# One tile for nine weight buffers, with the feature-major weights 16 bytes further on

## Chip, core and metric

The kernel runs as one program on one core of a Trainium2 chip. The metric is the device time of one execution in microseconds; for the kernel before it is the median of three runs.

## What is computed

Two transformer blocks in fp32 for 256 tokens of width 2048. Nearly all of the work is matrix products of the 256 tokens with weights that are read once from HBM:

```python
# first block
h = rmsnorm(x, g_mix);  proj = h @ w_in
y_sb = stick_breaking_attention(...);  y_ca = chunked_relpos_attention(...)
merged = sigmoid(gate_sb) * (y_sb @ w_sb_out) + sigmoid(gate_ca) * (y_ca @ w_ca_out)
x = x + merged @ w_mix_out
h = rmsnorm(x, g_ffn);  g_ff, u_ff = split(h @ w_ffn_in)
x = x + (silu(g_ff) * u_ff) @ w_ffn_out
x = x + sigmoid(rmsnorm(x, g_ple) @ w_ple_gate) * (p @ w_ple_in)
# second block: s5, gated linear attention and differential attention side by side,
# merged through w_out, then a gated MLP with a convolution (w_up, w_down), a last rmsnorm
```

## The kernel before

**Precision.** Every large product is made of three passes in `float32r`. Weights and activations are each split into a high part (rounded to `float32r`) and a low part (the rest), and high by high, high by low and low by high are summed in PSUM.

**Halves.** All weights pass through one loop, `stream` (L450). A half is 128 x 1024 fp32 of a weight matrix, 512 KB; there are 1089. For each half a DMA on SP's queue fills one of four `raw` buffers (L460), ScalarE writes the high part `wh` (L467), and VectorE writes the low part `wl` (L477). The step of half `i` first issues the cast of half `i + 4` and the subtraction of half `i + 3`, which in its turn issues the load of the half that comes four after its own; then it issues the matmuls of half `i`, and then one tick of the generators that do everything else (attention, norms, evacuations). `wh` has five buffers and `wl` four, each 4 KB per partition, each pool's buffers side by side.

**Two kinds of job.** The activations lie as `x`: for each block of 128 features, 256 columns of high parts and then 256 of low parts (2048 bytes per partition).

- In a token-major job (kind "AS", `mm_as`, L561 to L563) the activations are the stationary operand (128 x 128, 512 bytes per partition) and the weights are moved through, 512 columns at a time. A half of it has twelve matmuls: low activations by `wh`, high by `wl`, high by `wh`, for two feature blocks and two blocks of tokens.
- In a feature-major job (kind "WS", L527 and L531) a 128 x 128 piece of the weights is stationary and the activations are moved through: `wh` against all 512 columns of `x` (L527, the high matmul), `wl` against its 256 high columns only (L531, the low matmul). A half has sixteen matmuls, in pairs of a low and a high one; a job has four halves, so 32 pairs. The feature-major matrices are the query and key projections, `w_fin`, `w_up`, `w_u` and `w_r`: 492 of the halves. They come in runs of 16 to 48 halves, with token-major halves between.

A single half (`w_alr`, kind "W4") is 128 x 512 and is used in plain fp32.

**Memory.** Pools lie one behind the other in SBUF: the activation slots, the pool `one` (with the parameters `par` in it, and behind them the constants `cst`), then `raw`, `wh`, `wl` and the scratch pool `ev`. `par` has 208 columns and is given 96 more that nothing uses. In the layout that follows from these sizes, each of the five `wh` and four `wl` buffers starts 256 bytes away, modulo 512, from where each 2048-byte block of activations starts.

Of the kernel before, what the change touches and what calls it, by code (L numbers as in the profile page):

```python
# [9 lines left out]
F32 = mybir.dt.float32  # L10
F32R = mybir.dt.float32r
# [12 lines left out]
CA = 4  # L24
SA = 3
COOL = 1
RAWB = 4


# [130 lines left out]
class Flag:  # L160


    def __init__(self, tile=None):
        self.tile, self.ready = tile, False
# [21 lines left out]
class Build:  # L186
    NSLOT = 15

    def __init__(self, tc, d, out, es):
        self.tc, self.nc, self.d, self.out = tc, tc.nc, d, out  # L190
        pool = lambda name, bufs, **kw: es.enter_context(tc.tile_pool(name=name, bufs=bufs, **kw))
        self.slotp, self.one = pool("slots", 1), pool("one", 1)
        self.rawp, self.whp, self.wlp = pool("raw", RAWB), pool("wh", CA + 1), pool("wl", SA + 1)
        self.ev = pool("ev", 2)
        self.accp = pool("acc", 2, space=PSUM)
        self.psp = pool("ps", 1, space=PSUM)
        self.drp = pool("dr", 1, space=bass.MemoryType.DRAM)
        self.psfree, self.cooling, self.ticks = [0, 1, 2, 3], [], 0
        self.slotfree = list(range(self.NSLOT))
        self.gens, self.lanes, self.nm = [], {}, 0  # L200
        self.tab, self.forced, self.nrb = None, 0, 0
# [43 lines left out]
    def unbank(self, b):  # L245
        self.cooling.append((self.ticks + COOL, b[1]))

# [201 lines left out]
    def stream(self, jobs):  # L449
        nc = self.nc  # L450
        halves = [(j, i, ks) for j in jobs for i, ks in j.halves]
        N = len(halves)
        raws, spl = {}, {}
        width = lambda j, ks: {"AS": 512 * len(ks), "WS": 1024, "W4": 512}[j.kind]

        def load(i):
            j, idx, ks = halves[i]
            n = width(j, ks)
            r = self.rawp.tile([128, 1024], F32, tag="raw", name=self.name("raw"))
            nc.sync.dma_start(out=r[:, :n], in_=self.d[j.w][idx][:, :n])  # L460
            raws[i] = r

        def high(i):
            j, idx, ks = halves[i]
            n = width(j, ks)
            wh = self.whp.tile([128, 1024], F32R, tag="wh", name=self.name("wh"))
            nc.scalar.copy(wh[:, :n] if j.kind != "W4" else wh[:, :n].bitcast(F32), raws[i][:, :n])  # L467
            spl[i] = wh

        def low(i):  # L470
            j, idx, ks = halves[i]
            n = width(j, ks)
            r, wh = raws.pop(i), spl[i]
            wl = None
            if j.kind != "W4":
                wl = self.wlp.tile([128, 1024], F32R, tag="wl", name=self.name("wl"))
                nc.vector.tensor_sub(wl[:, :n], r[:, :n], wh[:, :n].bitcast(F32))  # L477
            spl[i] = (wh, wl)
            if i + RAWB < N:
                load(i + RAWB)  # L480

        ahead = self.at_start(load)
        for i in range(CA):
            next(ahead)
            high(i)
            if i < SA:
                low(i)
        self.add(ahead)
        last, prev, acc = None, None, None
        for i, (j, idx, ks) in enumerate(halves):  # L490
            if i + CA < N:
                high(i + CA)
            if i + SA < N:
                low(i + SA)
            if j is not last:
                if j.before is not None:
                    j.before()
                while prev is not None and not prev.free:
                    self.tick(must=True)
                prev, last = last, j  # L500
                acc = self.accp.tile([128, 2, 512], F32, tag="acc", name=self.name("acc"))
            for k in ks:
                while k not in j.acts.ready:
                    self.tick(must=True)
            first, end = j.halves[0][1][0], j.halves[-1][1][-1]
            if j.by_m is not None:

                for m in range(2):
                    for q, (_, _, kq) in enumerate(halves[i:]):
                        self.mm_as(j.acts, kq, *spl[i + q], acc, (m,), first, end)  # L510
                    j.by_m(m, acc)
                break
            wh, wl = spl.pop(i)
            if j.kind == "AS":
                self.mm_as(j.acts, ks, wh, wl, acc, (0, 1), first, end, low_last=i == 0)
            elif j.kind == "W4":

                for k in range(16):
                    p = slice(32 * (k % 4), 32 * (k % 4) + 32)
                    nc.tensor.matmul(acc[p, 0, :], lhsT=wh[:, 32 * k:32 * k + 32].bitcast(F32),  # L520
                                     rhs=j.acts.at(k).bitcast(F32), start=k < 4, stop=k >= 12)
            else:
                for kk, k in enumerate(ks):
                    x = j.acts.at(k)
                    for f in range(2):
                        s = slice((kk * 2 + f) * 128, (kk * 2 + f) * 128 + 128)
                        hi = lambda: nc.tensor.matmul(  # L527
                            acc[:, f, :], lhsT=wh[:, s], rhs=x, start=k == first, stop=k == end)
                        if k == first:
                            hi()  # L530
                        nc.tensor.matmul(acc[:, f, 256:512], lhsT=wl[:, s], rhs=x[:, 0:256], start=False, stop=False)  # L531
                        if k != first:
                            hi()
            if i + 1 == N or halves[i + 1][0] is not j:
                self.add(j.evac(acc, lambda j=j: setattr(j, "free", True)), front=True)
            self.tick()
        while self.gens:
            self.tick(must=True)
# [40 lines left out]
    def consts(self):  # L579
        nc, d, one = self.nc, self.d, self.one  # L580

        self.par = one.tile([128, P_N + 96], F32, tag="par", name="par")[:, 0:P_N]
        self.cst = one.tile([128, C_N], F32, tag="cst", name="cst")
        nc.sync.dma_start(out=self.par, in_=d["par"])
        c = self.cst
        self.ident, self.ones, self.BT = (c[:, o:o + 128] for o in (C_ID, C_ONE, C_BT))
        self.one1 = c[:, C_ONE:C_ONE + 1]
# [14 lines left out]
    def first(self):  # L602
# [6 lines left out]
        def start(load):  # L609
# [4 lines left out]
            def load_xt(g):  # L614
                nc.sync.dma_start(out=xs[g // 4][0][:, (g % 4) * 2:(g % 4) * 2 + 2], in_=d["xt"][:, 2 * g:2 * g + 2])

            for g in range(RAWB):
                load_xt(g)
                load(g)
            for k in range(16):  # L620
                if k % 2 == 0 and k // 2 + RAWB < 8:
                    load_xt(k // 2 + RAWB)
                if k == 8:
# [1146 lines left out]
```

## Time and profile before

| | us |
|---|---|
| median of three runs | 3164.16 |
| lowest and highest of them | 3163.18, 3164.53 |
| the profiled execution's own time | 3164.05 |
| its span, from the first to the last instruction | 3162.2 |

The page gives for each engine its busy time and number of instructions, the chain of work that ended last, and groups of instructions by line with the mean duration of one. Matmuls overlap (each is shown from its start to a modelled end, and the next starts before that), so a group's mean duration is not what one matmul costs: that is read from start to start in the timeline. "PEld" is the weight load that belongs to each matmul. The granted clock of TensorE is 0.999 of its full 2.4 GHz over the span.

### The profile page before, as it was taken

To read this page: it belongs to the slowest core of one execution; us is meant where nothing else is said; L and a number is where in the kernel's file an instruction comes from. 1 tells how busy PE (TensorE), PEld (TensorE's weight loads), DVE (VectorE), ACT (ScalarE), POOL (GpSimd) and SP (SyncE) were. 2 spreads that over 40 slices of the span, in tenths; PEclk is the share of its full clock that TensorE was granted. 3 is DMA by queue.
4 is the path that set the end of the run, shared out by engine and by line. 5 is a ranking of instruction groups with operands and counts; after the bars stand their busy time and mean duration, and the time that the engine had idled before them with its cause. 6 is when DMAs were issued, how large, how long until landed. Compare 5 with 4: busy or idle time off the path is not lost.

```text
span 3162.2 us, 43735 instructions
## 1 busy us (share of the span) xinstructions
PE 3143.5 (99%) x16909; PEld 2669.4 (84%) x16909; DVE 1993.3 (63%) x2593; ACT 1553.2 (49%) x2035; POOL 72.5 (2%) x158
## 2 busy tenths in 40 slices
PE   8999999999999999999999999999999999999998
PEld 7888888888888888888888888888888888888887
DVE  5656445557576676566655667945555766757666
ACT  6544444455444454456544454434445644545545
POOL 0000000000001000000000001000000000000000
PEclk9999999999999999999999999999999999999999
DMA  7455555555667666555654565655555565565555
GB/s 263 169 179 167 187 193 187 187 185 187 212 222 246 244 223 240 183 176 197 212 177 159 170 215 193 213 186 199 199 187 186 181 195 187 186 198 183 191 187 166
DMA packets 172640, 617.90 MB, mean 195 GB/s; under 512 B 23553, under 2 KB 23969, under 8 KB 169233
## 3 DMA queue, kind: packets, MB, share of 16 engines
q1 hardware_dynamic: 164992, 577.49, 55.1%
q0 software_dynamic: 7440, 37.64, 3.5%
q8 instruction: 132, 2.16, 0.3%
q14 instruction: 76, 0.61, 0.1%
HBM read 599.74 MB, written 14.25 MB: 194 GB/s over the span
## 4 chain that ended last, share of the span: by engine, by line
PE 99%; ACT 0%; DMA 0%; DVE 0%; DVEq 0%; issue 0%; SPq 0%; ACTq 0%
PE acc L527 29%; PE acc L561 17%; PE acc L563 17%; PE acc L562 17%; PE acc L531 15%; PE p L346 1%; PE p L1675 0%; PE p L1134 0%; PE p L1715 0%; PE p L908 0%; PE p L910 0%; PE p L909 0%; PE p L1718 0%; PE p L1111 0%; PE p L1130 0%; PE p L1709 0%
## 5 line engine op out<-in xcount | busy, mean ns | idle before, releaser
L477 DVE TENSOR_TENSOR wl<-raw,wh 128x1024 fp32r<-128x1024 f32 x1088 | 1320.2, 1220 | 649.9 <-PE acc L562 428.8
L467 ACT CAST wh<-raw 128x1024 fp32r<-128x1024 f32 x1088 | 1139.5, 1050 | 1092.5 <-PE acc L563 657.2
L527 PE MATMUL acc<-s,wh 128*128 128x512 f32 x3936 | 1385.2, 398 | 0.0
L531 PE MATMUL acc<-s,wl 128*128 128x256 f32 x3936 | 1090.7, 282 | 0.0
L561 PE MATMUL acc<-wh,s 128*128 128x512 f32 x2372 | 933.3, 393 | 0.8 <-DVE big L1353 0.8
L563 PE MATMUL acc<-wh,s 128*128 128x512 f32 x2372 | 925.0, 390 | 0.0
L562 PE MATMUL acc<-wl,s 128*128 128x512 f32 x2372 | 924.5, 390 | 0.0
L527 PEld LDWEIGHTS acc<-s,wh 128*128 128x128 f32 x3936 | 735.6, 188 | 165.0
L531 PEld LDWEIGHTS acc<-s,wl 128*128 128x128 f32 x3936 | 744.6, 189 | 11.0 <-issue 1.0
L561 PEld LDWEIGHTS acc<-wh,s 128*128 128x128 f32 x2372 | 446.0, 188 | 92.6 <-issue 1.7
L563 PEld LDWEIGHTS acc<-wh,s 128*128 128x128 f32 x2372 | 445.6, 188 | 92.9
L562 PEld LDWEIGHTS acc<-wl,s 128*128 128x128 f32 x2372 | 446.1, 188 | 91.0 <-issue 0.5
L443 DVE TENSOR_TENSOR s<-acc,s 128x512 f32<-128x512 f32 (+1 forms) x120 | 82.7, 690 | 273.9 <-ACT s L442 273.9
L442 ACT COPY s<-acc 128x512 f32<-128x512 f32 (+1 forms) x120 | 70.1, 584 | 196.6 <-PE acc L527 194.6
L310 ACT ACTIVATE s<-s 128x256 f32<-128x256 f32 (+4 forms) x175 | 76.6, 443 | 105.1 <-DVE s L313 38.2
L313 DVE SCALAR_TENSOR_TENSOR s<-s,conv 128x256 f32<-128x256 f32 x172 | 79.4, 482 | 3.4 <-ACT s L310 0.3
L445 DVE TENSOR_TENSOR s<-s,rb 128x512 f32<-128x512 f32 (+1 forms) x104 | 71.7, 690 | 3.5
L318 ACT CAST s<-s 128x256 fp32r<-128x256 f32 (+1 forms) x104 | 45.5, 441 | 30.4 <-DVE s L948 15.3
L1632 DVE TENSOR_TENSOR s<-s,s 128x1024 f32<-128x1024 f32 x48 | 58.5, 1219 | 0.0
L310 ACT ACTIVATE s<-s,conv 128x256 f32<-128x256 f32 x86 | 47.1, 595 | 22.0 <-DVE s L445 22.0
L319 DVE TENSOR_TENSOR s<-s,s 128x256 fp32r<-128x256 f32 (+1 forms) x104 | 47.5, 459 | 13.8 <-ACT s L318 12.5
L310 ACT ACTIVATE junk<-big 128x512 f32<-128x512 f32 x48 | 30.3, 632 | 49.5 <-DVE big L927 35.1
(265 smaller groups left out, 1036.8 us busy)
## 6 DMA issues: line engine op xcount, KB each, us to landing
raw<-in_w_fin SPq DMA_DIRECT2D x176, 512.0 KB, 4.3
raw<-in_w_up SPq DMA_DIRECT2D x172, 512.0 KB, 3.8
raw<-in_w_fout SPq DMA_DIRECT2D x88, 512.0 KB, 4.3
raw<-in_w_down SPq DMA_DIRECT2D x84, 512.0 KB, 4.1
raw<-in_w_qksb SPq DMA_DIRECT2D x32, 512.0 KB, 3.5
raw<-in_w_qkca SPq DMA_DIRECT2D x32, 512.0 KB, 3.3
raw<-in_w_gsb SPq DMA_DIRECT2D x32, 512.0 KB, 3.3
raw<-in_w_gca SPq DMA_DIRECT2D x32, 512.0 KB, 4.2
```

Source lines behind the costliest of these rows:

```text
L310: self.nc.scalar.activation(out, in_, func, scale=scale, **kw)
L313: self.nc.vector.scalar_tensor_tensor(out=out, in0=in0, scalar=scalar, in1=in1, op0=op0, op1=op1)
L442: nc.scalar.copy(out, acc[:, 0:n, 256:512])
L443: nc.vector.tensor_add(out, acc[:, 0:n, 0:256], out)
L445: nc.vector.tensor_mul(out, out, rb.tile[:, None, :].to_broadcast([128, n, 256]) if n > 1 else rb.tile[:, None, :])
L467: nc.scalar.copy(wh[:, :n] if j.kind != "W4" else wh[:, :n].bitcast(F32), raws[i][:, :n])
L477: nc.vector.tensor_sub(wl[:, :n], r[:, :n], wh[:, :n].bitcast(F32))
L527: hi = lambda: nc.tensor.matmul(acc[:, f, :], lhsT=wh[:, s], rhs=x, start=k == first, stop=k == end)
L531: nc.tensor.matmul(acc[:, f, 256:512], lhsT=wl[:, s], rhs=x[:, 0:256], start=False, stop=False)
L561: nc.tensor.matmul(acc[:, m, :], lhsT=xl, rhs=wh[:, s], start=k == first, stop=False)
L562: nc.tensor.matmul(acc[:, m, :], lhsT=xh, rhs=wl[:, s], start=False, stop=False)
L563: nc.tensor.matmul(acc[:, m, :], lhsT=xh, rhs=wh[:, s], start=False, stop=k == end)
```

## The change

1. The five `wh` and four `wl` buffers become slices of one tile `W`: five of 1024 columns, a gap of 64 columns (256 bytes), four of 1024, and 4 columns more.
2. The slices of feature-major halves start 4 columns (16 bytes) further on, those of token-major halves do not. Since a shifted slice reaches 16 bytes into the next one, `places` shifts a half only if it lies in the last slice of its row or the half after it is shifted too. At the end of each feature-major run some halves stay unshifted: 28 of 492 in `wh`, 6 of 492 in `wl`.
3. Where a shifted half reaches into a slice that still holds an unshifted half, its cast (41 times) or its subtraction (33 times) is issued behind the matmuls of the step instead of ahead of them. The first 16 bytes of the neighbour are read by the first half of its matmuls, so the write then waits for six matmuls more than before.
4. The weights of the one "W4" half go to a scratch tile of `ev` in plain fp32.
5. `par` gets 32 unused columns instead of 96. Everything behind it, up to the `wh` slices, lies 256 bytes lower; the gap of 64 columns puts the `wl` slices back where the `wl` buffers were.

On all five engines the queues hold the same instructions in the same order as before, row for row; only tile names, addresses and what some of the casts and subtractions wait for are different.

```diff
+WSH = 4
+GAP = 64
...
-        self.rawp, self.whp, self.wlp = pool("raw", RAWB), pool("wh", CA + 1), pool("wl", SA + 1)
+        self.rawp, self.wp = pool("raw", RAWB), pool("w", 1)
...
+        W = self.wp.tile([128, (CA + 1) * 1024 + GAP + (SA + 1) * 1024 + WSH], F32R, tag="w", name="w")
+
+        def places(first, bufs):
+            far = [False] * (N + 1)
+            for i in reversed(range(N)):
+                far[i] = halves[i][0].kind == "WS" and (far[i + 1] or i % bufs == bufs - 1)
+            at = [first + i % bufs * 1024 + WSH * far[i] for i in range(N)]
+            return at, {i for i in range(bufs, N) if far[i] and i % bufs != bufs - 1 and not far[i - bufs + 1]}
+
+        at_h, late_h = places(0, CA + 1)
+        at_l, late_l = places((CA + 1) * 1024 + GAP, SA + 1)
...
-            wh = self.whp.tile([128, 1024], F32R, tag="wh", name=self.name("wh"))
-            nc.scalar.copy(wh[:, :n] if j.kind != "W4" else wh[:, :n].bitcast(F32), raws[i][:, :n])
+            wh = W[:, at_h[i]:at_h[i] + 1024]
+            if j.kind == "W4":
+                wh = self.ev.tile([128, 512], F32, tag="b", name=self.name("w4"), bufs=1)
+            nc.scalar.copy(wh[:, :n], raws[i][:, :n])
...
-                wl = self.wlp.tile([128, 1024], F32R, tag="wl", name=self.name("wl"))
+                wl = W[:, at_l[i]:at_l[i] + 1024]
...
-            if i + CA < N:
+            if i + CA < N and i + CA not in late_h:
                 high(i + CA)
-            if i + SA < N:
+            if i + SA < N and i + SA not in late_l:
                 low(i + SA)
...
+            if i + CA in late_h:
+                high(i + CA)
+            if i + SA in late_l:
+                low(i + SA)
...
-        self.par = one.tile([128, P_N + 96], F32, tag="par", name="par")[:, 0:P_N]
+        self.par = one.tile([128, P_N + 32], F32, tag="par", name="par")[:, 0:P_N]
```

## Rows read from the trace of the kernel before

**Rows 1.** The page, part 1: busy time of each engine, its share of the span, instructions.

```profile
PE 3143.5 (99%) x16909; PEld 2669.4 (84%) x16909; DVE 1993.3 (63%) x2593; ACT 1553.2 (49%) x2035; POOL 72.5 (2%) x158
```

**Rows 2.** The waits of TensorE, all of them: who waited for whom, us in total, times, longest.

```profile
PE acc L553 <- ACT wh L467: 8.4, 1, 8.4
PE acc L561 <- DVE big L1353: 0.8, 1, 0.8
```

**Rows 3.** The page, part 4: the chain of work that ended last, by engine and by line.

```profile
PE 99%; ACT 0%; DMA 0%; DVE 0%; DVEq 0%; issue 0%; SPq 0%; ACTq 0%
PE acc L527 29%; PE acc L561 17%; PE acc L563 17%; PE acc L562 17%; PE acc L531 15%; PE p L346 1%; PE p L1675 0%; PE p L1134 0%; PE p L1715 0%; PE p L908 0%; PE p L910 0%; PE p L909 0%; PE p L1718 0%; PE p L1111 0%; PE p L1130 0%; PE p L1709 0%
```

**Rows 4.** The page, part 5: the matmuls of the stream, feature-major (L527, L531) and token-major (L561 to L563).

```profile
L527 PE MATMUL acc<-s,wh 128*128 128x512 f32 x3936 | 1385.2, 398 | 0.0
L531 PE MATMUL acc<-s,wl 128*128 128x256 f32 x3936 | 1090.7, 282 | 0.0
L561 PE MATMUL acc<-wh,s 128*128 128x512 f32 x2372 | 933.3, 393 | 0.8 <-DVE big L1353 0.8
L563 PE MATMUL acc<-wh,s 128*128 128x512 f32 x2372 | 925.0, 390 | 0.0
L562 PE MATMUL acc<-wl,s 128*128 128x512 f32 x2372 | 924.5, 390 | 0.0
```

**Rows 5.** The chain in order of time (start us, us, what) in a run of `w_up`: the place where two high matmuls follow each other comes once in each feature-major job, near its start, so from one of these rows to the next is one job of 32 pairs.

```profile
2466.03 0.46 PE acc L527 x2
...
2477.32 0.46 PE acc L527 x2
...
2488.60 0.46 PE acc L527 x2
```

**Rows 6.** The timeline of TensorE inside one of these `w_up` jobs (start us, us, engine, line, operation, tiles).

```profile
2478.44 0.28 PE L531 MATMUL acc<-s,wl 128*128 128x256 f32 x1
2478.55 0.40 PE L527 MATMUL acc<-s,wh 128*128 128x512 f32 x1
2478.79 0.28 PE L531 MATMUL acc<-s,wl 128*128 128x256 f32 x1
2478.91 0.39 PE L527 MATMUL acc<-s,wh 128*128 128x512 f32 x1
2479.13 0.28 PE L531 MATMUL acc<-s,wl 128*128 128x256 f32 x1
2479.25 0.40 PE L527 MATMUL acc<-s,wh 128*128 128x512 f32 x1
2479.48 0.28 PE L531 MATMUL acc<-s,wl 128*128 128x256 f32 x1
2479.60 0.40 PE L527 MATMUL acc<-s,wh 128*128 128x512 f32 x1
2479.84 0.28 PE L531 MATMUL acc<-s,wl 128*128 128x256 f32 x1
2479.96 0.40 PE L527 MATMUL acc<-s,wh 128*128 128x512 f32 x1
```

**Rows 7.** The timeline of TensorE in a job of the projection `w_r`: the first and the last of 18 high matmuls, each with its low one between.

```profile
1535.03 0.40 PE L527 MATMUL acc<-s,wh 128*128 128x512 f32 x1
...
1540.92 0.39 PE L527 MATMUL acc<-s,wh 128*128 128x512 f32 x1
```

**Rows 8.** The timeline of TensorE in a token-major job: a matmul and the weight load that stands beside it; then the first and the last of 25 matmuls that follow each other.

```profile
1499.91 0.39 PE L563 MATMUL acc<-wh,s 128*128 128x512 f32 x1
1499.91 0.19 PEld L561 LDWEIGHTS acc<-wh,s 128*128 128x128 f32 x1
1500.14 0.39 PE L561 MATMUL acc<-wh,s 128*128 128x512 f32 x1
...
1505.58 0.39 PE L561 MATMUL acc<-wh,s 128*128 128x512 f32 x1
```

**Rows 9.** The page, part 5: the subtraction and the cast, and what ended most of the idle time before them.

```profile
L477 DVE TENSOR_TENSOR wl<-raw,wh 128x1024 fp32r<-128x1024 f32 x1088 | 1320.2, 1220 | 649.9 <-PE acc L562 428.8
L467 ACT CAST wh<-raw 128x1024 fp32r<-128x1024 f32 x1088 | 1139.5, 1050 | 1092.5 <-PE acc L563 657.2
```

**Rows 10.** The page, part 6: the loads of the two longest feature-major matrices; KB each, us from issue to landing.

```profile
raw<-in_w_fin SPq DMA_DIRECT2D x176, 512.0 KB, 4.3
raw<-in_w_up SPq DMA_DIRECT2D x172, 512.0 KB, 3.8
```

**Rows 11.** The groups by line and shape: the transposes that read the constants `cst`.

```profile
L346 PE MATMUL p<-cst,big 128*128 128x128 f32 x128 | 16.6, 273 | 0.0
L346 PE MATMUL p<-cst,s 128*128 128x128 f32 x64 | 8.5, 276 | 0.0
```

More of the change, by code (lines that the diff above doesn't have):

```diff
@@ L519, in stream @@
                     p = slice(32 * (k % 4), 32 * (k % 4) + 32)
-                    nc.tensor.matmul(acc[p, 0, :], lhsT=wh[:, 32 * k:32 * k + 32].bitcast(F32),
+                    nc.tensor.matmul(acc[p, 0, :], lhsT=wh[:, 32 * k:32 * k + 32],
                                      rhs=j.acts.at(k).bitcast(F32), start=k < 4, stop=k >= 12)
```

## The prediction

> **What bounds the kernel.** I read the busy shares first: TensorE is busy for 3143.5 of 3162.2 us, VectorE 63% and ScalarE 49% of the span [rows 1]. Then its waits: two in the whole execution, 9.2 us together, both outside the steady stream [rows 2]. Then the chain that ended last, which is TensorE for 99%: 29 + 15% of it in the two feature-major lines, 3 x 17% in the three token-major ones [rows 3]. So nobody makes TensorE wait, and a change gains or loses only by altering how many nanoseconds lie between one matmul's start and the next.
>
> That spacing is not what the columns alone give. At 2.4 GHz and one column a cycle, 512 columns take 213.3 ns and 256 take 106.7. A token-major matmul has 512: 24 of them take 1505.58 - 1500.14 = 5.44 us, 226.7 ns each, 13.3 more than the columns [rows 8]. A feature-major pair has 768 columns, 320 ns: a job of 32 pairs takes 2477.32 - 2466.03 = 11.29 and then 11.28 us, 352.7 ns a pair, 32.7 more [rows 5]. Two matmuls lie in a pair, so it pays 16.3 per matmul where token-major work pays 13.3. And a pair does not always cost the same. Within one job the time from one high matmul to the next is 0.36, 0.34, 0.35, 0.36 us, uneven though the work is equal [rows 6]; in a `w_r` job 17 pairs take 1540.92 - 1535.03 = 5.89 us, 346.5 ns each [rows 7]. Same shapes, same line numbers, 6.2 ns less, and 346.5 is 320 plus 2 x 13.3. So something beside the columns delays TensorE, and it can settle into a better and a worse rhythm. What runs beside each matmul is the weight load of the next, which starts in the same hundredth of a microsecond [rows 8]: two reads of SBUF at once, at addresses that the layout sets. The change moves just these addresses.
>
> **The change, part by part.**
>
> *The 16 bytes, on feature-major halves.* 3936 pairs [rows 4]. No row shows a pair with another offset, so its price is bounded. Below: no delay at all, 320 ns a pair, 3936 x 32.7 ns = -129 us. Above: a rhythm worse than the present one; the longest pair in the rows is 0.36 against 0.3527, 3936 x 7.3 = +29 us if every pair took it. Between these ends I take the better rhythm that the rows already show, 346.5 ns, because it is the nearest row: same instructions, one delay of 13.3 ns per matmul, as in token-major work. `w_fin` and `w_up` have 176 and 172 halves [rows 10], 87 jobs of 32 pairs: 87 x 32 x 6.2 = -17.3 us. The other 144 halves, 36 jobs, stand among attention work and are partly in the better rhythm already; I count half of their 36 x 32 x 6.2 = 7.1, -3.6 us. Sum -20.9 us. The 28 high and 6 low halves that stay unshifted are some 3% of the 984 parts and take back less than 1 us.
>
> *The high weights 256 bytes lower.* The gap puts the low weights back in place, but the high ones now start at the same offset modulo 512 as the activations, where they stood 256 bytes off. Token-major matmuls with high weights are 2 x 2372 = 4744 [rows 4]. No row has that offset. Below: the 13.3 ns vanish, -63 us. Above: each gets the longest spacing that a high feature-major matmul shows, 0.24 us against 0.2267 [rows 6], +13.3 ns, +63 us. I take zero: the three token-major lines keep one spacing although their operands are 512, 1024 and 2048 bytes apart, so most offsets make no difference there.
>
> *The late writes.* 41 casts and 33 subtractions wait for six matmuls more, 6 x 226.7 ns = 1.36 us. The cast takes 1.05 and the subtraction 1.22 us [rows 9]. A half of twelve token-major matmuls lasts 2.72 us, and the cast is issued for a half four steps ahead, so of some 3.5 x 2.72 = 9.5 us the delay and both writes take 3.6. Behind a late cast on ScalarE stand evacuations and the next casts; these casts already sit idle for 657 us in all until a matmul releases a buffer [rows 9], and TensorE does not notice [rows 2]. On SP's queue the load that follows a late subtraction is issued up to 1.36 us later; it lands in 4.3 us [rows 10], and its cast is issued three steps, some 8 us, later. Cost: nothing. If that cover were gone, 41 x 1.36 = 56 us, all at the seams between runs.
>
> *One tile, the scratch tile, `par`.* The releases of the nine slices are still those of the matmuls that read them, and the queues hold the same rows in the same order: nothing. The one W4 cast into scratch happens once: nothing. The constants lie 256 bytes lower; the transposes that read them are 16.6 + 8.5 = 25.1 us [rows 11], and 5% of it either way is 1.3 us: nothing taken.
>
> Sum: the profiled execution's own 3164.05 - 20.9 = **3143 us**. That execution lies 0.11 us under the median of 3164.16, so no correction.
>
> The Trainium skill speaks against this gain. Its page "TensorE: Matmul & The Clock Gate", section "Step-by-step: what each phase is for", says that the moving operand and the weight load have read ports of their own and that loading the next weights doesn't steal read bandwidth from the running matmul; by that rule an address shift changes nothing and the time stays at 3164. The trace leans against it, with two rhythms of equal work, but does not show that addresses are the cause.
>
> **Rivals.**
>
> 1. *The delay goes much further down.* For it: the smallest spacings in the rows are 0.22 for a high matmul (2478.91 to 2479.13) and 0.11 for a low one (2478.44 to 2478.55), 0.33 together [rows 6], so a pair can run nearly at column speed. Against: the two never stand side by side in these rows. At 0.33 us for all pairs: 3936 x 22.7 ns = -89, 3075 us. Its own range is 3035 (all of the 129) to 3120.
> 2. *No change.* The reads of the two operands don't meet by address; the extra time is a fixed price of swapping the weights, and the two rhythms come from something else, such as the phase in which the sequence starts. For it: token-major work shows one spacing for every offset it has [rows 8], and the worse rhythm returns in job after job, 11.29 and 11.28 us [rows 5]. Then 3164, within some 5 us.
> 3. *Slower, by the token-major matmuls.* Place: L561 and L563 of before, the 4744 matmuls that move high weights, whose start now coincides modulo 512 with the activations being loaded. Price: if the coincidence throws them into the worse rhythm, whose surplus over the better one is 6.2 per pair, 3.1 ns a matmul, 4744 x 3.1 = +14.7 us, and with the feature-major gain absent 3179 us. It decides from 1.3 ns a matmul on (6.3 us). Against: 256 bytes is half of the 512 by which these operands already differ among themselves without effect. With the full 13.3 ns it would be 3227.
>
> **How the numbers follow.** 0.2% is 6.3 us, about what a measurement of this kernel can tell from no change. The forecast, a better rhythm (3120 to 3157), gets 0.34; the deeper gain 0.26; no change 0.24; slower 0.16. So faster 0.60, same 0.24, slower 0.16. The most likely time is 3143. The range leaves out about the lower third of the deeper gain (0.09), and of the slower case what lies beyond 3181 (0.08): 3065 to 3181. Cases of both signs lie in it; the likeliest one's own range is 3120 to 3157.
>
> **What would show it.** Right: one feature-major job in `w_up` takes about 11.09 us instead of 11.29 from row to row of the chain, evenly spaced pairs near 346 ns, token-major matmuls still at 226.7, and no new wait of TensorE. Rival 1: jobs at 10.6 us. Rival 2: 11.29 again. Rival 3: token-major spacing at 229 or more where high weights move. The prediction is wrong if the token-major lines move by more than 1 ns, if TensorE waits for casts at the seams between runs, or if pairs fall well under 346 ns.

## The result and the profile after

| | before | after |
|---|---|---|
| time, median of 4 | 3163.82 us (3163.18 to 3164.53) | 3147.96 us (3147.50 to 3149.19) |
| span of the profiled execution | 3162.2 us | 3146.6 us |
| ratio after / before | | 0.9950, 95% interval 0.9933 to 0.9968 |

The change makes the kernel 15.9 us faster; the forecast was 20.9 us faster, 3143 us, with a range of 3065 to 3181. The interval lies wholly below 1, and 0.5% is more than the 0.2% that a measurement of this kernel can tell from no change.

What stood first in the reading of before is unchanged. Busy times of the page after, part 1 (against [rows 1]):

```profile
PE 3128.3 (99%) x16909; PEld 2665.2 (85%) x16909; DVE 1993.2 (63%) x2593; ACT 1553.2 (49%) x2035; POOL 72.5 (2%) x158
```

The waits of TensorE after (against [rows 2]; who waited for whom, us in total, times, longest):

```profile
PE acc L575 <- ACT w L485: 8.1, 1, 8.1
PE acc L583 <- DVE big L1375: 0.8, 1, 0.8
```

The chain that ended last, by engine and line (against [rows 3]):

```profile
PE 99%; ACT 0%; DMA 0%; DVE 0%; DVEq 0%; issue 0%; SPq 0%; ACTq 0%
PE acc L545 29%; PE acc L583 17%; PE acc L584 17%; PE acc L585 17%; PE acc L549 15%; PE p L348 1%; PE p L1697 0%; PE p L1156 0%; PE p L1737 0%; PE p L930 0%; PE p L932 0%; PE p L931 0%; PE p L1740 0%; PE p L1133 0%; PE p L1152 0%; PE p L1731 0%
```

TensorE still bounds the kernel with the same number of instructions, waits for the same two things, and is busy 15.2 us less. VectorE, ScalarE and GpSimd are where they were to 0.1 us. The late writes made no new wait, and the idle times of subtractions and casts are within 1 us of those in [rows 9]:

```profile
L495 DVE TENSOR_TENSOR w<-raw,w 128x1024 fp32r<-128x1024 f32 x1088 | 1320.1, 1220 | 649.5 <-PE acc L584 431.1
L485 ACT CAST w<-raw 128x1024 fp32r<-128x1024 f32 x1088 | 1138.5, 1049 | 1093.4 <-PE acc L585 663.9
```

The 15 us are in one line. The matmul groups after, part 5 of the page (against [rows 4]; busy us, mean ns of one, idle time before):

```profile
L545 PE MATMUL acc<-s,w 128*128 128x512 f32 x3936 | 1369.4, 393 | 0.0
L549 PE MATMUL acc<-s,w 128*128 128x256 f32 x3936 | 1090.4, 282 | 0.0
L583 PE MATMUL acc<-w,s 128*128 128x512 f32 x2372 | 932.2, 393 | 0.8 <-DVE big L1375 0.8
L585 PE MATMUL acc<-w,s 128*128 128x512 f32 x2372 | 923.8, 389 | 0.0
L584 PE MATMUL acc<-w,s 128*128 128x512 f32 x2372 | 923.6, 389 | 0.0
```

The high feature-major matmuls fell from 1385.2 to 1369.4 us; the low ones (1090.7 to 1090.4) and the three token-major lines (933.3, 925.0 and 924.5 before) moved by about 1 us at most. Since matmuls overlap, the sum that counts is from each start to the next start, over all matmul records of the trace, added up by the line of the first: feature-major 1391.9 us before and 1376.2 after, token-major 1626.5 and 1627.0. The difference of the first, -15.8 us, is the whole gain.

Inside `w_up`, the chain in order of time after (against [rows 5]; from row to row is one job of 32 pairs):

```profile
2457.25 0.46 PE acc L545 x2
...
2468.36 0.46 PE acc L545 x2
...
2479.48 0.46 PE acc L545 x2
```

11.11 us a job instead of 11.29. And TensorE's timeline inside such a job after (against [rows 6]):

```profile
2463.69 0.39 PE L545 MATMUL acc<-s,w 128*128 128x512 f32 x1
2463.92 0.28 PE L549 MATMUL acc<-s,w 128*128 128x256 f32 x1
2464.04 0.39 PE L545 MATMUL acc<-s,w 128*128 128x512 f32 x1
...
2467.85 0.39 PE L545 MATMUL acc<-s,w 128*128 128x512 f32 x1
```

Twelve pairs in 4.16 us are 346.7 ns each, the pair of [rows 7], and now even: 0.23 us from a high matmul to its low one, 0.12 from there to the next high one, pair after pair. Token-major work after (against [rows 8]) has 18 matmuls from the first of these rows to the last, 4.08 us, 226.7 ns each, as before:

```profile
1494.95 0.39 PE L583 MATMUL acc<-w,s 128*128 128x512 f32 x1
...
1499.03 0.39 PE L583 MATMUL acc<-w,s 128*128 128x512 f32 x1
```

### The profile page after: what moved, and what is told of

The parts are those of the page before. It is cut to its first block, busy times and chain, and to the rows that moved or that the text cites. A ratio compares the mean times of both kernels' runs of the same rounds, so it can differ in the third digit from the quotient of the medians.

```text
span 3146.6 us, 43726 instructions
## 1 busy us (share of the span) xinstructions
PE 3128.3 (99%) x16909; PEld 2665.2 (85%) x16909; DVE 1993.2 (63%) x2593; ACT 1553.2 (49%) x2035; POOL 72.5 (2%) x158
## 4 chain that ended last, share of the span: by engine, by line
PE 99%; ACT 0%; DMA 0%; DVE 0%; DVEq 0%; issue 0%; SPq 0%; ACTq 0%
PE acc L545 29%; PE acc L583 17%; PE acc L584 17%; PE acc L585 17%; PE acc L549 15%; PE p L348 1%; PE p L1697 0%; PE p L1156 0%; PE p L1737 0%; PE p L930 0%; PE p L932 0%; PE p L931 0%; PE p L1740 0%; PE p L1133 0%; PE p L1152 0%; PE p L1731 0%
## 5 line engine op out<-in xcount | busy, mean ns | idle before, releaser
L495 DVE TENSOR_TENSOR w<-raw,w 128x1024 fp32r<-128x1024 f32 x1088 | 1320.1, 1220 | 649.5 <-PE acc L584 431.1
L485 ACT CAST w<-raw 128x1024 fp32r<-128x1024 f32 x1088 | 1138.5, 1049 | 1093.4 <-PE acc L585 663.9
L545 PE MATMUL acc<-s,w 128*128 128x512 f32 x3936 | 1369.4, 393 | 0.0
L549 PE MATMUL acc<-s,w 128*128 128x256 f32 x3936 | 1090.4, 282 | 0.0
L583 PE MATMUL acc<-w,s 128*128 128x512 f32 x2372 | 932.2, 393 | 0.8 <-DVE big L1375 0.8
L585 PE MATMUL acc<-w,s 128*128 128x512 f32 x2372 | 923.8, 389 | 0.0
L584 PE MATMUL acc<-w,s 128*128 128x512 f32 x2372 | 923.6, 389 | 0.0
L545 PEld LDWEIGHTS acc<-s,w 128*128 128x128 f32 x3936 | 733.4, 188 | 153.1
L549 PEld LDWEIGHTS acc<-s,w 128*128 128x128 f32 x3936 | 740.2, 188 | 10.4 <-issue 1.0
L585 PEld LDWEIGHTS acc<-w,s 128*128 128x128 f32 x2372 | 445.4, 188 | 94.0
L583 PEld LDWEIGHTS acc<-w,s 128*128 128x128 f32 x2372 | 445.6, 188 | 93.1 <-issue 1.7
L584 PEld LDWEIGHTS acc<-w,s 128*128 128x128 f32 x2372 | 445.6, 188 | 91.0 <-issue 0.5
L320 ACT CAST s<-s 128x256 fp32r<-128x256 f32 (+1 forms) x104 | 45.7, 443 | 29.5 <-DVE s L970 14.3
```

The lines of the kernel that those rows point to most:

```text
L485: nc.scalar.copy(wh[:, :n], raws[i][:, :n])
L545: hi = lambda: nc.tensor.matmul(acc[:, f, :], lhsT=wh[:, s], rhs=x, start=k == first, stop=k == end)
L583: nc.tensor.matmul(acc[:, m, :], lhsT=xl, rhs=wh[:, s], start=k == first, stop=False)
L584: nc.tensor.matmul(acc[:, m, :], lhsT=xh, rhs=wl[:, s], start=False, stop=False)
L585: nc.tensor.matmul(acc[:, m, :], lhsT=xh, rhs=wh[:, s], start=False, stop=k == end)
```

## The experiments

Theory: the gain comes from where the feature-major weights start, and from nothing else in the edit. The rivals are that another part brings it (the one tile, the 256 bytes, the writes that come later), and, among theories of the address, several forms: it is the weights alone or the distance between the two operands, only a step upward helps, or every operand has good and bad starts of its own. All kernels are the changed one with the edit shown. e1 is the median of ten executions and e2 of four; e3 to e12 ran once each. Before, timed beside them, took 3163.88 us (e1 to e4, median of 13), 3163.42 (e5 to e8, one) and 3163.35 (e9 to e12, one). In the table, "feature" and "token" are the sums from start to start, in us, got as above. They tell more than the single times do: before, after, e1, e3, e4, e6, e7 and e8 have token-major sums from 1626.1 to 1627.0, and after, e2, e4, e5 and e10 feature-major sums from 1376.1 to 1376.6.

| | edit to the changed kernel | feature | token | time, us |
|---|---|---|---|---|
| before | | 1391.9 | 1626.5 | 3163.82 |
| after | | 1376.2 | 1627.0 | 3147.96 |
| e1 | no shift at all | 1392.3 | 1626.4 | 3163.52 |
| e2 | token-major halves shifted too | 1376.1 | 1659.1 | 3179.88 |
| e3 | high feature-major weights alone | 1392.1 | 1626.5 | 3162.73 |
| e4 | low feature-major weights alone | 1376.3 | 1626.6 | 3147.47 |
| e5 | feature-major +16 B, token-major -16 B | 1376.6 | 1686.7 | 3208.15 |
| e6 | shift of 32 B | 1382.3 | 1626.7 | 3154.02 |
| e7 | shift of 8 B | 1381.5 | 1626.8 | 3153.44 |
| e8 | shift of -16 B | 1446.1 | 1626.1 | 3226.31 |
| e9 | activations +16 B, weights unshifted | 1379.5 | 1660.4 | 3189.46 |
| e10 | activations and all weights +16 B | 1376.3 | 1653.0 | 3180.23 |
| e11 | all behind `par` 128 B lower | 1385.7 | 1665.4 | 3195.90 |
| e12 | all behind `par` 64 B lower | 1384.5 | 1670.6 | 3200.01 |

### Which part of the edit does it: e1 to e4

**e1_no_shift**

```diff
-WSH = 4
+WSH = 0
```

> The changed kernel with the shift set to zero columns: one tile, the high weights still 256 bytes lower, no 16 bytes. Theory (the 16 bytes against the activations make the rhythm): feature-major jobs are back at 11.29 us from row to row of the chain, pairs at 352.7 ns and uneven, time 3163 to 3165 us. Rival A (the 256 bytes by which the high weights moved do it): jobs stay near 11.12 us, pairs 347 ns, time 3147 to 3150. Rival B (the late writes or the one tile do it): also 3147 to 3150 as far as the tile does it.

Measured: 3163.52 us, ratio to before 0.9999 (0.9990 to 1.0008). The one tile, the scratch tile, the late writes (`places` picks the same halves for them), the other `par` and the 256 bytes between rows of slices together bring and cost nothing; with all of them and no shift, the job is back at 11.29 us. e1's chain in order of time, in `w_up`:

```profile
2476.32 0.46 PE acc L545 x2
...
2487.61 0.46 PE acc L545 x2
```

**e2_all_shifted**

```diff
-                far[i] = halves[i][0].kind == "WS" and (far[i + 1] or i % bufs == bufs - 1)
+                far[i] = True
```

> All halves, the token-major ones too, start 16 bytes further on; no half is written late. Theory (only the distance of the two reads modulo a small number of bytes matters): feature-major pairs at 347 ns as in the changed kernel; token-major matmuls, which have no uneven rhythm to lose, stay at 226.7 ns, time 3146 to 3150 us; then the late writes and the two places are not needed. Rival (token-major work is spoiled by the shift): token-major matmuls at 228 ns or more, 7116 x 1.3 ns = +9 us or more, time above 3156.

Measured: 3179.88 us, ratio to before 1.0050 (1.0034 to 1.0067). The feature-major sum keeps its gain, the token-major one pays 32.1 us more than after, 4.5 ns for each of its 7116 matmuls. e2's timeline in a token-major job, from the first to the last of 24:

```profile
2640.07 0.40 PE L583 MATMUL acc<-w,s 128*128 128x512 f32 x1
...
2645.63 0.40 PE L583 MATMUL acc<-w,s 128*128 128x512 f32 x1
```

231.7 ns each instead of 226.7, with all TensorE waits as after (8.1 and 0.8 us). So the rule that gives the shift to feature-major halves alone is worth 32 us. It also shows that the 34 halves which the rule leaves unshifted don't matter: with them shifted, the feature-major sum is the same.

**e3_high_only** and **e4_low_only**: `places` gets an argument that keeps one of the two rows of slices unshifted.

```diff
+        def places(first, bufs, on=1):
+                far[i] = bool(on) and halves[i][0].kind == "WS" and (far[i + 1] or i % bufs == bufs - 1)
# e3
+        at_l, late_l = places((CA + 1) * 1024 + GAP, SA + 1, 0)
# e4
+        at_h, late_h = places(0, CA + 1, 0)
```

> Only the high parts of feature-major halves are shifted by 16 bytes, the low parts are not. Theory (the uneven rhythm needs a delay in the short low matmul, beside which the high weights are loaded): high only is enough, pairs at 347 ns, time near 3148 us. Rival (the load of the low weights beside the long high matmul is what is late): pairs at 352.7 ns, time near 3164. If both loads count alike, a value between, about 350 ns and 3156.

> Only the low parts of feature-major halves are shifted by 16 bytes. Theory (the high weights, loaded beside the short low matmul, decide): pairs stay at 352.7 ns, time near 3164 us. Rival (the low weights, loaded beside the long high matmul, decide): pairs at 347 ns, time near 3148. If both count alike: about 350 ns, 3156.

Measured: 3162.73 and 3147.47 us. The low weights alone bring all of it, the high ones nothing that these runs show. e4's chain in order of time has the job of after, 11.11 us:

```profile
2456.21 0.47 PE acc L545 x2
...
2467.32 0.47 PE acc L545 x2
```

The load of the low weights (L531) starts together with a high matmul (L527), 512 columns long; the high ones are loaded beside a low matmul of 256 columns. The timeline of before, in `w_up`:

```profile
2467.27 0.40 PE L527 MATMUL acc<-s,wh 128*128 128x512 f32 x1
2467.27 0.19 PEld L531 LDWEIGHTS acc<-s,wl 128*128 128x128 f32 x1
```

The 41 late casts are not needed for the gain, and leaving them out saves nothing either (0.5 us, single run). e3's timeline in `w_up` tells one thing more:

```profile
2480.73 0.40 PE L545 MATMUL acc<-s,w 128*128 128x512 f32 x1
2480.97 0.28 PE L549 MATMUL acc<-s,w 128*128 128x256 f32 x1
2481.08 0.40 PE L545 MATMUL acc<-s,w 128*128 128x512 f32 x1
...
2483.91 0.40 PE L545 MATMUL acc<-s,w 128*128 128x512 f32 x1
```

Nine pairs in 3.18 us are 353.3 ns each, as slow as before, but even: 0.24 and 0.12, where [rows 6] go 0.36, 0.34, 0.35. In these jobs, shifting the high weights removed the unevenness and not the cost: uneven pairs and slow pairs are two things.

### Direction and size of the step: e5 to e8

**e5_token_minus16**

```diff
-WSH = 4
+WSH = 8
+BASE = 4
...
+            at = [first + BASE + i % bufs * 1024 + WSH * far[i] for i in range(N)]
...
-        self.par = one.tile([128, P_N + 32], F32, tag="par", name="par")[:, 0:P_N]
+        self.par = one.tile([128, P_N + 24], F32, tag="par", name="par")[:, 0:P_N]
```

> Token-major halves start 16 bytes lower than in the changed kernel, feature-major ones stay 16 bytes further on (a lead of 4 columns in the tile, 8 unused columns fewer in par, a shift of 8 columns). Since in token-major work the weights are the moving operand, 16 bytes less there put the stationary operand 16 bytes further on relative to the moving one, the sign that helped feature-major work. Theory (the sign of the distance decides): token-major matmuls stay at 226.7 ns or fall, time 3148 us or less. Rival (any 16 bytes off the 256-byte raster spoil token-major work): uneven at some 231 ns as with the shift of all halves, time near 3180.

Measured: 3208.15 us. The feature-major sum is that of after, the token-major one is 59.7 us longer, more than for +16 bytes (32.1). e5's timeline in a token-major job, 23 matmuls:

```profile
2640.19 0.40 PE L584 MATMUL acc<-w,s 128*128 128x512 f32 x1
...
2645.55 0.40 PE L586 MATMUL acc<-w,s 128*128 128x512 f32 x1
```

5.36 / 23 = 233.0 ns each. This is one of the faster stretches: 59.7 us over 7116 matmuls are 8.4 ns for each of them.

**e6_shift_32** (`WSH = 8`) and **e7_shift_8** (`WSH = 2`)

> The shift is 8 columns, 32 bytes, instead of 16. Theory (it is enough that the loaded low weights lie a little further on than the activations being moved): pairs at 347 ns or less, time 3140 to 3150 us. Rival (what counts is an odd number of 16-byte lines between the two): as without the shift, 352.7 ns, 3164.

> The shift is 2 columns, 8 bytes, half of 16. Theory (lines of 16 bytes count): no whole line further, and the loads straddle lines, so between 3148 and 3170 us; as without the shift (352.7 ns a pair, 3164) if only whole lines count. Rival (a delay that grows smoothly with the bytes): half of the effect, 350 ns, 3156.

Measured: 3154.02 and 3153.44 us, feature-major sums 9.6 and 10.4 us under that of before, so some six tenths of the gain of 16 bytes. In e6 most pairs have the 346.7 ns of after, and in some jobs pairs of 240 + 121 ns stand among them; in e7 many jobs run in a steady cycle of three pairs (235, 231 and 228 ns to the low matmul, 118 from there on), 349.3 ns on average. So neither theory of these two runs holds: 32 bytes are not as good as 16, and 8 bytes bring more than half.

**e8_shift_minus16**: feature-major weights 16 bytes lower than the token-major ones.

```diff
-WSH = 4
+WSH = -4
+BASE = 8
...
-                far[i] = halves[i][0].kind == "WS" and (far[i + 1] or i % bufs == bufs - 1)
+                far[i] = halves[i][0].kind == "WS"
...
-            return at, {i for i in range(bufs, N) if far[i] and i % bufs != bufs - 1 and not far[i - bufs + 1]}
+            return at, set()
```

> Feature-major halves start 16 bytes lower instead of further on (no late writes; at the seams between runs the first shifted half overwrites four columns of a weight still to be used). Theory (the sign decides): pairs slower than unshifted or equal, 352.7 ns or more, time 3164 to 3190 us. Rival (any 16 bytes off the raster help feature-major work): 347 ns, 3148.

Measured: 3226.31 us, 63 us slower than before, which taken alone would have spoken for "only upward". The waits of TensorE in e8, without the two that after has too, show most of what it is (L546 and L550 are the high and the low feature-major matmul):

```profile
PE acc L550 <- DVE w L496: 36.6, 30, 3.5
PE acc L546 <- ACT w L486: 21.7, 14, 3.9
```

These 58.3 us in 44 waits are new. They stand at the start of three or four of the last four halves of each run of feature-major halves. There the cast and the subtraction of token-major halves, issued four and three steps ahead, fill unshifted slices, and the last 16 bytes of such a slice lie on the first 16 of the lower feature-major slice behind it, whose matmuls come later in the order of the code. So TensorE waits for the write, and then reads 16 bytes that belong to another half: e8 computes something else there, and its times alone count here. At the other end of the runs, where the expectation has the overlap, no wait appears.

The granted clock is 0.50 (the 1.2 GHz level) in three stretches, one behind each of the three longest of these waits. Before the first of them TensorE had stood still for 3.1 us, and then four pairs take 0.64 us each. In the change, with its rule of places and its late writes, none of these waits and stretches appears.

Away from the seams the lower start helps too; e8's timeline in `w_up`:

```profile
2525.92 0.39 PE L546 MATMUL acc<-s,w 128*128 128x512 f32 x1
...
2528.70 0.39 PE L546 MATMUL acc<-s,w 128*128 128x512 f32 x1
```

Eight pairs in 2.78 us, 347.5 ns each. The whole trace says less. Take the time from one high matmul to the next with a low one between, without the few of 420 ns or more, and its mean in each of the 13 runs of feature-major halves. In the eight runs of `w_fin` and `w_up`, before has 351.8 to 352.7 ns, after 347.3 and e8 347.5 to 348.3. In the five other runs, before has 347.8 to 351.2, after 347.2 to 347.8 and e8 348.9 to 350.8. So in the long matrices a step down does nearly what a step up does, and in the others it does not, which no run explains.

In e5 and e8, `raw` and the constants also lie 32 bytes lower than in after. In e8, where the token-major weights stand where they do in after, the token-major sum is 1626.1 us, so this move costs that work nothing, and it is not what slows e5.

### Weights, activations or the distance between them: e9 to e12

**e9_x_plus16**: the activations start 16 bytes further on, the weights where they were before.

```diff
-WSH = 4
+WSH = 0
+XSH = 4
-    NSLOT = 15
+    NSLOT = 14
-        return self.slotp.tile(shape, dtype, tag=f"s{i}", name=self.name("s")), i
+        t = self.slotp.tile([128, 2048 + 128], dtype, tag=f"s{i}", name=self.name("s"))[:, XSH:XSH + n]
...
```

> The activations start 16 bytes further on in their slots and no weight is shifted (slots 512 bytes longer, 14 of them instead of 15). The weights then lie 16 bytes lower relative to the activations, as in the two runs with minus 16. Theory R (only the distance between the two operands counts): feature-major pairs 347 ns (all of them together 1376 us), token-major matmuls some 236 ns (1687 us). Rival A (each operand's own start counts: a shifted moving operand spoils token-major work, a shifted stationary one helps feature-major work): here the weights stand on their raster, so token-major matmuls stay at 226.7 ns (1627 us) and pairs at 352.7 (1392 us). The time itself may be a few us off by the slot that is missing.

**e10_both_plus16**: the same, and all halves of the weights 16 bytes further on too (`WSH = 4`, `far[i] = True`), so that the distance between the operands is that of before.

> The activations and all weights start 16 bytes further on (14 longer slots as in the run before). Theory R (only the distance counts): as without any shift, pairs 352.7 ns (1392 us), token-major matmuls 226.7 ns (1627 us). Rival A (each operand's own start counts): as with all weights shifted, pairs 347 ns (1376 us), token-major matmuls 231 ns (1659 us).

Measured: 3189.46 and 3180.23 us. The slot that is missing costs a little of its own: both have two new waits of TensorE (3.2 us together), and e9 then 6.8 and e10 10.2 us at a granted clock of 0.50. In e9 the feature-major sum falls by 12.4 us though no weight is shifted, so it is not the weights' own start that is bad. In e10 the distance is that of before, and yet the feature-major sum is that of after and the token-major one is 26.5 us longer than before; so it is not the distance alone. e10's timeline in a token-major job, 24 matmuls:

```profile
2639.77 0.39 PE L589 MATMUL acc<-w,s 128*128 128x512 f32 x1
...
2645.29 0.39 PE L589 MATMUL acc<-w,s 128*128 128x512 f32 x1
```

230.0 ns each. In e9 token-major matmuls take 226.7 ns in some stretches and some 233 in most, with the same weights' starts in both, which no run explains.

**e11_minus128** and **e12_minus64**: all that lies behind `par`, so `raw` and the weights among the rest, 128 or 64 bytes lower.

```diff
# e11
+        self.par = one.tile([128, P_N + 0], F32, tag="par", name="par")[:, 0:P_N]
# e12
+        self.par = one.tile([128, P_N + 16], F32, tag="par", name="par")[:, 0:P_N]
```

> The changed kernel with par given no unused columns: the whole tile lies 128 bytes lower, the 16 bytes stay. High and low weights are then 128 bytes off where they were 0 and 256. Theory (a raster of 128 bytes or a divisor of it): token-major matmuls at 226.7 ns, pairs at 347, time 3147 to 3149 us. Rival (a raster of 256 bytes): token-major matmuls uneven and slower, 231 to 237 ns, 3180 to 3215 us. It can also show a distance that is better than both for token-major work: under 226 ns.

> As the run before with 64 bytes instead of 128 (16 unused columns in par). Theory (a raster of 64 bytes or a divisor of it): token-major matmuls at 226.7 ns, time 3147 to 3149 us. Rival (a raster of 128 or 256 bytes): token-major matmuls 231 to 237 ns, 3180 to 3215 us.

Measured: 3195.90 and 3200.01 us. The token-major sums grow by 38.4 and 43.6 us against after, and the feature-major ones lose 9.5 and 8.3 of the 15.8 us. e11's timeline in a token-major job, 24 matmuls:

```profile
2639.73 0.40 PE L583 MATMUL acc<-w,s 128*128 128x512 f32 x1
...
2645.32 0.39 PE L583 MATMUL acc<-w,s 128*128 128x512 f32 x1
```

232.9 ns each. So steps of 64 and 128 bytes cost the token-major work as much as one of 16 does.

**What stands after all runs.** Shown: the gain is the start of the low feature-major weights (e1, e3, e4). Token-major work has its 226.7 ns throughout only in the runs in which its activations start where they do before and its weights do too, or lie 256 bytes lower (the high ones of after), whatever the feature-major weights do; each of the six runs that moved either otherwise (e2, e5, e9 to e12) makes it 26 to 60 us longer. For feature-major work the starts of before are the worst that were tried (e1 and e3 equal them), and moving the low weights or the activations helps.

What the other engines do beside TensorE has no part in it that the traces show. In e2, a token-major matmul takes 231.9 ns to the next start while VectorE and ScalarE are idle (busy for under 5% of the interval; 2102 intervals) and 231.7 while both are busy (over 95%; 2090). In 191 of the first, with GpSimd idle and almost no DMA in flight too, it is 231.8. The same two cases give 226.9 and 226.9 before, and 235.5 and 235.6 in e5; the feature-major pairs of before give 351.4 (492) and 351.7 (987). So the slow spacing of token-major work is there with nobody else at work, and the slow pairs are there with VectorE and ScalarE idle.

Open: why. A rule by the weights' own start falls with e9, one by the distance alone with e10, one by the direction alone with e8. Both starts, that of the weights and that of the activations, enter; but every matmul of these runs has a weight load beside it, so none of them tells whether the two reads of TensorE delay each other or each of them is slower by itself from some starts.

## Why the prediction was right

**The bound.** TensorE with no waits to lose, so that only the spacing counts: right. The waits after are those of before, and the whole difference is in that spacing.

**The 16 bytes.** The place and the step held: the shift of feature-major weights brings their pairs from the worse rhythm to the better one, 346.5 ns by [rows 7], and the steady pairs after take 346.7. That these are two reads that meet, as the prediction has it, no run shows, and that only the low weights count it did not say. There was luck in it too: no row of before could show that 16 bytes reach the better rhythm in full. 8 and 32 bytes reach some six tenths of it (e6, e7), and 16 bytes less 128 or 64 under half (e11, e12). What was off is the size of both terms, by 5 us in all. `w_fin` and `w_up`: -17.3 forecast, -14.3 measured (-7.0 and -7.3, by the sums from start to start). A job fell from 11.29 to 11.11 us and not to 11.09: it takes 347.3 ns a pair on average, mostly since its first pairs are longer than the steady ones, which 32 x 346.5 left out. These 0.8 ns are 2.2 of the 3.0 us; the rest has no one place. After's timeline at the start of a job shows it:

```profile
2458.13 0.40 PE L545 MATMUL acc<-s,w 128*128 128x512 f32 x1
2458.36 0.28 PE L549 MATMUL acc<-s,w 128*128 128x256 f32 x1
2458.49 0.39 PE L545 MATMUL acc<-s,w 128*128 128x512 f32 x1
2458.72 0.28 PE L549 MATMUL acc<-s,w 128*128 128x256 f32 x1
2458.84 0.39 PE L545 MATMUL acc<-s,w 128*128 128x512 f32 x1
```

0.36 and then 0.35 us; further on the pairs settle at 346.7 ns. The other 36 jobs: -3.6 forecast as half of 7.1, -1.5 measured, so about a fifth: more of them ran in the better rhythm already than [rows 7] let one count. The 28 and 6 unshifted halves: less than 1 us, and e2 shows no difference at all.

**256 bytes lower.** Taken as zero between -63 and +63 us: right, the token-major sum moved by 0.5 us and e1 by nothing. The reason given, that most offsets make no difference there, does not hold. e11 and e12 cost 38 and 44 us with 128 and 64 bytes, and 16 bytes cost 32. The rows of before had only offsets that are multiples of 512 to compare; that 256 would be harmless did not follow from them, and the forecast was right on this term without having shown it.

**Late writes, one tile, scratch, `par`.** Nothing, right: waits and idle times are those of before to about 1 us, and e1, which has all four, is at 0.9999.

**The rivals.** Deeper gain: no run here has pairs that stay well under 346 ns; the smallest spacings of [rows 6], 0.22 and 0.11, remain the two parts of different pairs. No change: e1 to e4 show that the worse rhythm is a matter of addresses and no fixed price of swapping weights. The rule of the Trainium skill that stood for it, in "TensorE: Matmul & The Clock Gate", section "Step-by-step: what each phase is for", is that the weight load takes nothing from the running matmul's reads. What the prediction drew from it, that an address shift changes nothing, does not hold here: with the same instructions the kernel takes from 3148 to 3208 us by addresses alone, without a new TensorE wait (e5 against after). Whether the load takes from the matmul's reads, no run here shows. Slower by the token-major matmuls: its place was real, since these matmuls are the ones that lose most by a wrong offset, but the change's 256 bytes is an offset they tolerate. It decided from 1.3 ns a matmul on; after has 0.1, e2 4.5.

## What to carry to other kernels

Where one engine is busy 99% of the time and waits for nothing, compare the time from start to start of equal instructions in different stages: two rhythms for the same work (here 353 and 346.5 ns a pair) mean that something other than the work can be gained, and here the better one was the size of it. Which step of an address reaches it, only runs told. Take that gain only where it is: here one class of operands wants its start moved by 16 bytes, and the other loses twice as much by the same step. A layout change that moves everything behind a padded tile can cost more than the edit brings (e11 and e12: 48 and 52 us over after), so keep an experiment that undoes the shift alone.

## What the runs showed of the hardware

- The start of an SBUF operand changes the speed of a matmul stream without any wait in the profile: token-major matmuls of 512 columns take from 226.7 to some 233 ns each in the rows above, and a feature-major pair 346.7 or 353.3. The slower spacing is the same with VectorE and ScalarE idle or busy (e2: 231.9 and 231.7 ns).
- Sizes and directions don't add up to a simple rule: for the feature-major sum +16 bytes gave 15.8 us, +8 and +32 gave 10.4 and 9.6, and -16 gave pairs of 347.5 to 348.3 ns in `w_fin` and `w_up`, against 347.3 with +16; for the token-major sum -16 bytes cost 60 us and +16 cost 32.
- No run has steady stretches shorter, by more than the rounding of the rows, than some 346.5 ns a pair and 226.7 ns a token-major matmul: 13.3 ns per matmul over one column a cycle at 2.4 GHz, with a granted clock of 0.999 over the span.
